# RWKV-7 chunk inverse: a direct product for the transposed matrix, half-width f16 copies into block-diagonal operands, and a new instruction order

## The chip, the cores and the metric

The kernel runs on one core of one Trainium2 chip (trn2). The metric is the device time of one execution in microseconds, as the median of several runs. The core has four engines that matter here. PE is the matrix engine, whose weight loads are listed apart as PEld. DVE is the vector engine, ACT the scalar engine and POOL the general engine. SP issues the transfers. Each engine runs its own instructions in a fixed order, and semaphores hold an instruction back until what it reads is there.

## What is computed

One layer of a streaming encoder: a projection feeds four HGRN2 heads and eight RWKV-7 heads, then come an output projection, cross attention over 256 memory rows, a SwiGLU block and the final norm. 1024 prompt tokens and 32 sample tokens go through it. The change touches the RWKV-7 recurrence alone:

```python
def rwkv7_mixer(p, shift0, s0, mu, w0, w_b, a0, a_b, g_b, k_k, k_a, r_k, gn_w, gn_b):
    ...
    a = jax.nn.sigmoid(a0 + ad @ a_b)
    kk = k * k_k
    k = k * (1.0 + (a - 1.0) * k_a)
    ...
    kk = kk / jnp.maximum(jnp.sqrt(jnp.sum(kk * kk, axis=-1, keepdims=True)), 1e-12)

    def step(S, xs_t):
        r_t, w_t, k_t, v_t, kk_t, a_t = xs_t
        sa = jnp.einsum('bhvk,bhk->bhv', S, -kk_t)
        S = (S * w_t[:, :, None, :] + sa[..., None] * (kk_t * a_t)[:, :, None, :]
             + v_t[..., None] * k_t[:, :, None, :])
        return S, jnp.einsum('bhvk,bhk->bhv', S, r_t)
```

The kernel computes it in chunks of 64 tokens. Inside a chunk the steps depend on each other through a strictly triangular 64x64 matrix A (token against token). The chunk needs the inverse of the identity minus A.

## The kernel before

The whole program is recorded as a graph (`Graph.record`) and laid out by a planner (`Graph.order`, `Graph.plan`) before it is emitted. So every instruction carries the line of the one emitting call, L384. The planner places instructions engine by engine. It uses estimated costs (`price`), a table of ranks, and perturbations of the ranks from the constants `START` and `NUDGE`. It packs buffers into regions of the on-chip memory: `f` and `mb` for most tiles, `r`, `rw` and `wr` for weights and rounded operands. These region names, and `bank` for the eight accumulator banks, are the names that a profile shows.

`mixers` runs `rwkv(0)`, two HGRN2 heads, `rwkv(2)` and two more HGRN2 heads. Beside them stand the projections that feed the second half, and later the key and value projections of the memory. The planner weaves these dense matmuls between the small ones, twelve at a time (`CUT = 4`, three matmuls each). `rwkv(j)` handles two pairs of heads (a pair fills the 128 partitions, 64 each) in five stages `s`. Four stages have 256 tokens, that is K = 8 chunks over the two pairs, and the last has 32 tokens and K = 2. That gives eight large stages and two small ones. One stage at a time may be in its first part (`AHEAD`, kind `rw`). A stage does the following.

- It forms the decayed operands. `ar[:, 0]` and `ar[:, 1]` hold the key direction and the receptance. `kbk[:, c, e]` holds, for head half e, the key direction times a, and the other slot holds k. The factor on k is formed by two tensor-scalar operations on POOL (`ka`, `oka`), followed by a multiply on POOL.
- Products of A: for each chunk and head half one f32 matmul, with 64 rows of weights, 128 columns of output and 128 moving columns (both parts of `ar` at once). It gives A, the k part of it, and the same for the receptance. DVE evacuates them through a mask in eight instructions of 256 columns into `am` and `aq`.
- `inverse(am, K)`: 16 small matmuls against the identity transpose A. DVE subtracts the result from the identity into the block-diagonal f32 tile `abd`, ACT copies that to f16 (`a16`), and POOL makes the first `xbd` from it. Then come five levels of doubling on f16 operands. In each, PE multiplies `a16` by y. DVE masks the result into p (`self.levs`, 512 columns) and again, twice as wide and with the zero halves, into the block-diagonal `pbd` (`place`, 1024 columns from the accumulator). PE multiplies `xbd` by p (the new y, copied by ACT) and `pbd` by x. DVE places that into `xbd`, again 1024 columns wide, and ACT copies it to x. At level 1 the product with x is made from both halves of `xbd` (`product_diag`, 16 matmuls in place of 8). A last f32 product corrects the result.
- The second part of the stage (kind `rc`) runs over its chunks one after another and ends with the group norm.

What the change touches: the constants at L38, `price` (L238 to L269), the masks in `constants`, the tile `diag` in `mixers`, the two `ka` instructions and the products of A in `rwkv`, and `inverse`.

Of the kernel before, what the change touches and what calls it, by code (L numbers as in the profile page):

```python
# [11 lines left out]
F32 = mybir.dt.float32  # L12
# [25 lines left out]
START, NUDGE = (3607, 1), ((80, 4396, 3), (130, 3947, 0.6), (150, 4396, 3), (265, 8110, 6), (275, 4333, 1.5), (340, 8895, 0.6), (380, 3280, 3), (405, 8085, 0.6), (410, 6339, 6), (420, 6614, 3), (430, 156, 0.2), (730, 4743, 12), (845, 2394, 1.5), (865, 156, 0.2), (870, 6104, 12), (875, 4027, 6), (895, 4109, 0.6), (900, 2031, 12), (905, 8539, 12), (930, 7618, 3), (950, 8689, 3), (965, 6104, 12), (975, 8050, 3), (985, 6104, 12), (1045, 8604, 12), (1060, 5136, 12), (1070, 4495, 1.5), (1255, 1, 0), (1295, 1462, 3), (1365, 8029, 1.5), (1430, 8194, 3), (1470, 9186, 0.2), (1530, 8029, 1.5), (1560, 8200, 1.5), (1630, 7663, 12), (1640, 7326, 3), (1700, 5100, 3), (1725, 629, 12), (1755, 5100, 3), (1760, 1728, 3), (1775, 4762, 6),)  # L38
# [188 lines left out]
def price(eng, method, args, kw):  # L227
# [39 lines left out]
    if method == "tensor_scalar":  # L267
        return 0.24 + n * (3.3e-3 if args[4] == ALU.max else 1.1e-3), 0.0
# [440 lines left out]
class Net:  # L709
# [5 lines left out]
    def constants(self):  # L715
# [33 lines left out]
        both = self.both = c.tile([128, 2, 64], F32, name="both")  # L749
        nc.vector.tensor_copy(both.rearrange("p h u -> p (h u)"), j64)  # L750

        def diagonal(m):

            d = c.tile([128, 2, 64], F32, name="levd")
            nc.vector.tensor_tensor(d, m.unsqueeze(1).to_broadcast([128, 2, 64]), both, ALU.mult)
            return d


        self.lev, self.levs = [], []
        for l in range(6):  # L760
# [10 lines left out]
            self.lev.append(diagonal(m) if l else m)  # L771
        self.lev0y = self.lev[0]
# [8 lines left out]
        self.lev0x = diagonal(m).rearrange("p h u -> p (h u)")  # L781
# [716 lines left out]
    def mixers(self):  # L1498
# [138 lines left out]
    def rwkv(self, j):  # L1637
# [8 lines left out]
        for s in range(5):  # L1646
# [72 lines left out]
            for a in range(2):  # L1719
                G.tensor_scalar(of(a_, a), of(a_, a), self.P("ka", j + a), self.P("oka", j + a), ALU.mult, ALU.add)  # L1720
# [13 lines left out]
            am, aq = ([self.w(t).rearrange("p (c u) -> p c u", c=8)[:, :K] for _ in half] for t in ("am", "aq"))  # L1734
# [26 lines left out]
            y1 = self.inverse(am, K)  # L1761
            akv = self.w("akv").rearrange("p (c u) -> p c u", c=8)[:, :K]
            ps = self.psm.tile([128, 8, 64], F32, tag="m", name="ps_ak")[:, :K]
            for c in range(K):
                PE.matmul(ps[0:64, c], lhsT=am[0][64:128, c], rhs=z[64:128, c, 0], start=True, stop=True)
                PE.matmul(ps[64:128, c], lhsT=am[1][0:64, c], rhs=z[0:64, c, 1], start=True, stop=True)
# [85 lines left out]
    def inverse(self, am, nc_):  # L1852
# [9 lines left out]
        abd = self.diag[self.diag_n % DIAG][:, :nc_]  # L1862
        self.diag_n += 1
        a16, xbd, pbd = (self.tmp([128, 8, 128], t, F16)[:, :nc_] for t in ("a16", "xbd", "pbd"))
# [14 lines left out]
        def product_diag(left, right):  # L1879

            ps = stacked()
            for c in range(nc_):
                PE.matmul(ps[:, c], lhsT=left[:, c], rhs=right[:, c, 0:64], start=True, stop=False)
                PE.matmul(ps[:, c], lhsT=left[:, c], rhs=right[:, c, 64:128], start=False, stop=True)
            nc.cut()
            return ps

        def halves_product(left, right):

            ps = stacked()  # L1890
            for c in range(nc_):
                for hf in half:
                    PE.matmul(ps[hf, c], lhsT=left[hf, c, hf], rhs=right[hf, c], start=True, stop=True)
# [209 lines left out]
```

## Time and profile before

| | |
|---|---|
| Three timed runs | 1793.56, 1795.97, 1800.94 us; median 1795.97 us |
| Span of the profiled execution, first to last instruction | 1792.9 us |
| Mean granted PE clock | 0.996 |
| Mixers (RWKV, HGRN2, projections, memory keys and values) | from about 95 to about 740 us of the span |
| Matmul records | 15639; f32 matmuls that are no transposes leave two records each |

The files give no time of the profiled execution other than its span, so sums are made against the 1792.9 us. The median of the runs is 3.1 us above that. A profile's group row reads: line, engine, operation, written tile and read tiles, shape, count, then the busy time in us and the mean of one in ns, then the idle time of the engine just before such instructions and who ended it. The mean length of a matmul is a latency, since matmuls overlap. What one costs is the busy time divided by the count.

### The profile page before, as it was taken

The page shows a single profiled execution, that of the slowest core. Times are in us where ns is not written, and L with a number is a line of the kernel's source. Part 1 is how long each engine was busy: PE and PEld are TensorE (multiplying, and loading weights), DVE is VectorE, ACT ScalarE, POOL GpSimd, SP SyncE. Part 2 cuts the span into 40 slices and gives each one's busy share as a digit, 9 for nine tenths or more (in the row PEclk, how much of TensorE's full clock was granted, in tenths as well). Part 3 has the DMA queues.
Part 4 walks back from the last instruction along what each step waited for, and adds up shares of the span by engine and source line. Part 5 has one row for each costly group of instructions (what it writes and reads, how often), then busy time and mean ns, then how long its engine had stood idle before and what let it go on. Part 6 is the DMA issues. An engine that isn't in the chain of part 4 may idle for free.

```text
span 1792.9 us, 39695 instructions
## 1 busy us (share of the span) xinstructions
PE 1753.3 (98%) x15639; PEld 1665.4 (93%) x15639; DVE 1289.6 (72%) x2538; ACT 854.3 (48%) x2025; POOL 575.1 (32%) x729
## 2 busy tenths in 40 slices
PE   7999999999999999999999999999999999999998
PEld 6998888898888888999999999999999999999997
DVE  6466668847768798424564557998777877979997
ACT  6745536656555677533333446333333333753432
POOL 5024325425524542153000037422322323233321
PEclk9999999999999999999999999999999999999999
DMA  5734323223412237743112233133222244645522
GB/s 186 226 110 113 108 63 97 79 85 97 120 56 68 60 92 246 240 138 105 48 49 70 90 115 96 57 123 114 90 98 98 95 141 152 184 142 158 185 84 98
DMA packets 212555, 205.06 MB, mean 114 GB/s; under 512 B 18808, under 2 KB 197616, under 8 KB 212368
## 3 DMA queue, kind: packets, MB, share of 16 engines
q1 hardware_dynamic: 212368, 202.52, 36.3%
q8 instruction: 123, 2.02, 0.5%
q14 instruction: 64, 0.52, 0.1%
HBM read 142.80 MB, written 59.67 MB: 113 GB/s over the span
## 4 chain that ended last, share of the span: by engine, by line
PE 79%; DVE 9%; ACT 3%; DMA 3%; POOL 3%; issue 3%; SPq 0%; DVEq 0%; ACTq 0%; POOLq 0%
PE bank L384 79%; DVE f L384 4%; DVE mb L384 2%; POOL f L384 1%; DVE rw L384 1%; DVE r L384 1%; ACT mb L384 1%; ACT f L384 1%; POOL mb L384 1%; DMA p_scratch<-mb 1%; DMA r<-h_scratch 1%; DMA mb<-in_x_prompt_dram 0%; ACT rw L384 0%; DMA f<-p_scratch 0%; DMA f<-out_dram 0%
## 5 line engine op out<-in xcount | busy, mean ns | idle before, releaser
L384 PE MATMUL bank<-r,rw 128*128 128x264 f32 (+1 forms) x5952 | 895.9, 305 | 1.5 <-DVE f L384 0.7
L384 PEld LDWEIGHTS bank<-r,rw 128*128 128x128 f32 x5952 | 840.3, 189 | 8.7 <-DVE rw L384 1.4
L384 PE MATMUL bank<-mb,rw 128*128 128x264 f32 (+3 forms) x3648 | 506.0, 293 | 2.7 <-ACT rw L384 0.9
L384 PEld LDWEIGHTS bank<-mb,rw 128*128 128x128 f32 x3648 | 481.2, 188 | 7.1 <-DVE rw L384 1.6
L384 DVE TENSOR_TENSOR f<-bank,f 128x264 f32<-128x264 f32 (+7 forms) x524 | 236.7, 466 | 161.1 <-PE bank L384 143.8
L384 ACT CAST rw<-wr 128x1024 fp32r<-128x1024 f32 (+3 forms) x168 | 119.7, 718 | 203.7 <-PE bank L384 176.8
L384 DVE TENSOR_TENSOR f<-f 128x264 f32<-128x264 f32 (+9 forms) x336 | 204.8, 628 | 13.4 <-ACT f L384 8.7
L384 POOL TENSOR_TENSOR f<-f 128x2 f32<-128x2 f32 (+8 forms) x201 | 112.6, 571 | 309.4 <-ACT f L384 260.6
L384 ACT ACTIVATE f<-f 128x256 f32<-128x256 f32 (+7 forms) x327 | 138.3, 445 | 119.8 <-DVE f L384 71.7
L384 PE MATMUL bank<-f 128*128 128x128 f32 (+13 forms) x1245 | 159.4, 275 | 4.6 <-DVE f L384 2.2
L384 DVE TENSOR_TENSOR mb<-bank,f 128x1024 f16<-128x1024 f32 (+5 forms) x191 | 135.3, 732 | 37.1 <-PE bank L384 32.2
L384 PEld LDWEIGHTS bank<-f 128*128 128x128 f32 (+5 forms) x1189 | 117.2, 159 | 24.0 <-DVE f L384 4.2
L384 DVE TENSOR_TENSOR rw<-wr,rw 128x512 fp32r<-128x512 f32 (+3 forms) x146 | 118.3, 816 | 28.1 <-ACT rw L384 24.3
L384 PE MATMUL bank<-f,mb 128*128 128x64 f16 (+5 forms) x2296 | 121.9, 218 | 15.8 <-DVE mb L384 14.2
L384 ACT CAST rw<-r 128x512 fp32r<-128x512 f32 (+2 forms) x111 | 63.2, 570 | 116.9 <-PE bank L384 90.6
L384 ACT COPY mb<-bank 128x512 f32<-128x512 f32 (+5 forms) x165 | 74.0, 462 | 70.2 <-PE bank L384 63.3
L384 ACT COPY f<-bank 128x264 f32<-128x264 f32 (+8 forms) x207 | 70.1, 356 | 53.5 <-PE bank L384 47.1
L384 DVE TENSOR_TENSOR rw<-r,rw 128x512 fp32r<-128x512 f32 (+2 forms) x111 | 77.7, 702 | 17.1 <-ACT rw L384 16.8
L384 PEld LDWEIGHTS bank<-f,mb 64*64 64x64 f32 (+4 forms) x1280 | 57.6, 140 | 30.5 <-DVE mb L384 16.2
L384 ACT CAST rw<-f 128x512 fp32r<-128x512 f32 (+3 forms) x71 | 45.9, 647 | 71.1 <-PE bank L384 64.6
L384 POOL TENSOR_TENSOR rw<-wr,rw 128x1024 fp32r<-128x1024 f32 x22 | 52.7, 2399 | 82.7 <-ACT rw L384 75.2
L384 PE MATMUL bank<-mb 64*64 64x64 f32 (+5 forms) x1516 | 73.4, 230 | 4.2 <-DVE mb L384 3.4
(121 smaller groups left out, 1818.8 us busy)
## 6 DMA issues: line engine op xcount, KB each, us to landing
wr<-in_w_in_dram SPq DMA_DIRECT2D x36, 512.0 KB
p_scratch<-mb SPq DMA_DIRECT2D x79, 176.0 KB
wr<-in_w_ff_dram SPq DMA_DIRECT2D x27, 512.0 KB
r<-in_w_ff_dram SPq DMA_DIRECT2D x25, 512.0 KB
f<-h_scratch SPq DMA_DIRECT2D x48, 264.0 KB
h_scratch<-f SPq DMA_DIRECT2D x16, 528.0 KB
f<-x_scratch SPq DMA_DIRECT2D x15, 528.0 KB
f<-p_scratch SPq DMA_DIRECT2D x60, 128.0 KB
```

Source lines behind the costliest of these rows:

```text
L384: getattr(eng, method)(*args, **kw)
```

## The change

Part by part:

- A is no longer made and then transposed. One set of 16 matmuls makes A transposed directly (`pst`, weights from `ar`, moving columns from `kbk`), and DVE copies it through a mask into `a32`, which starts as minus the identity (`copy_predicated`). A second set of 16 makes the k part (`psk`). A third, with 64 moving columns, makes the receptance part, first all chunks of one half, then all of the other (`pse`). Evacuations are 512 columns wide.
- `a32` is 64 columns wide per chunk. `xbd`, `pbd` and `abd` are three lasting f16 tiles, zeroed once. They are filled by two half-partition copies each: `a16` by ACT, `pbd` and `xbd` by DVE, from the f16 tiles p and x.
- `product_diag` is gone. x goes from the accumulator through ACT, and then by the two copies to `xbd`.
- The two `ka` instructions go to DVE.
- `price` gets entries for such copies and for POOL's tensor-scalar with two pointers. `START` and `NUDGE` get new numbers, so that the order of the whole program is another.

```diff
-START, NUDGE = (3607, 1), ((80, 4396, 3), (130, 3947, 0.6), (150, 4396, 3),
...
+START, NUDGE = (976, 1), ((20, 678, 0.6), (35, 5853, 0.6), (40, 8101, 3),
...
     if eng == "vector":
+        if method in ("tensor_copy", "tensor_scalar") and all(v.buf.space == "SB" for v in args[:2]):
+            return 0.135 + n * (0.26e-3 if out.dtype == args[1].dtype == F16 else 0.52e-3), 0.0
...
-        return 0.24 + n * (3.3e-3 if args[4] == ALU.max else 1.1e-3), 0.0
+        pointers = sum(isinstance(a, View) for a in args[2:])
+        return 0.24 + n * (3.3e-3 if args[4] == ALU.max else 4e-3 if pointers > 1 else 1.1e-3), 0.0
...
-            self.diag.append(self.sp.tile([128, 8, 128], F32, name="abd"))
-            nc.gpsimd.memset(self.diag[-1], 0.0)
+            self.diag.append(self.sp.tile([128, 8, 64], F32, name="a32"))
+            nc.vector.tensor_scalar(self.diag[-1], self.i64.unsqueeze(1).to_broadcast([128, 8, 64]), -1.0, None, ALU.mult)
+        self.bd = [self.sp.tile([128, 8, 128], F16, name=t) for t in ("xbd", "pbd", "abd")]
+        for t in self.bd:
+            nc.gpsimd.memset(t, 0.0)
...
             for a in range(2):
-                G.tensor_scalar(of(a_, a), of(a_, a), self.P("ka", j + a), self.P("oka", j + a), ALU.mult, ALU.add)
+                V.tensor_scalar(of(a_, a), of(a_, a), self.P("ka", j + a), self.P("oka", j + a), ALU.mult, ALU.add)
...
-            for a in range(2):
-                pse = [self.psm.tile([128, 4, 128], F32, tag="m", name="ps_a")[:, :m] for _ in half]
-                for c in range(m):
-                    for e, hf in enumerate(half):
-                        PE.matmul(pse[e][:, c], lhsT=kb[m * a + c][e], rhs=ar[hf, :, 64 * (m * a + c):64 * (m * a + c) + 64],
-                                  start=True, stop=True)
-                for e in range(2):
-                    for lst, o in ((am, 0), (aq, 64)):
-                        V.tensor_tensor(lst[e][:, m * a:m * a + m], pse[e][:, :, o:o + 64],
-                                        self.mask_a[:, o:o + 64].unsqueeze(1).to_broadcast([128, m, 64]), ALU.mult)
+            pst, psk, *pse = [self.psm.tile([128, 8, 64], F32, tag="m", name=t)[:, :K] for t in ("ps_at", "ps_am", "ps_aq", "ps_aq")]
+            a32 = self.diag[self.diag_n % DIAG][:, :K]
...
+                    PE.matmul(pst[hf, c], lhsT=ar[hf, 0, cc], rhs=kbk[hf, c, e], start=True, stop=True)
+            V.copy_predicated(a32, self.mask_t.unsqueeze(1).to_broadcast([128, K, 64]), pst)
...
+                    PE.matmul(psk[half[1 - e], c], lhsT=kbk[hf, c, 1 - e], rhs=ar[hf, 0, cc], start=True, stop=True)
+            V.tensor_tensor(am, psk, self.mask_a[:, 0:64].unsqueeze(1).to_broadcast([128, K, 64]), ALU.mult)
+            for e, hf in enumerate(half):
+                for c in range(K):
+                    PE.matmul(pse[e][:, c], lhsT=kb[c][e], rhs=ar[hf, 1, 64 * c:64 * c + 64], start=True, stop=True)
+                V.tensor_tensor(aq[e], pse[e], self.mask_a[:, 64:128].unsqueeze(1).to_broadcast([128, K, 64]), ALU.mult)
...
-        def place(dst, ps, mask):
-            V.tensor_tensor(dst.rearrange("p c (h u) -> p c h u", h=2),
-                            ps.unsqueeze(2).to_broadcast([128, nc_, 2, 64]),
-                            mask.unsqueeze(1).to_broadcast([128, nc_, 2, 64]), ALU.mult)
-
-        ps = stacked()
-        for c in range(nc_):
-            for e, hf in enumerate(half):
-                PE.matmul(ps[hf, c], lhsT=am[e][hf, c], rhs=self.ident[hf, hf], start=True, stop=True)
-        for hf in half:
-            V.tensor_tensor(abd[hf, :, hf], ps[hf], bc(self.i64[hf]), ALU.subtract)
+        def place(dst, src):
+            for hf in half:
+                V.tensor_copy(dst[hf, :, hf], src[hf])
+
...
-        S.copy(a16, abd)
-        G.tensor_tensor(xbd, abd, bc(self.lev0x), ALU.mult)
+        for hf in half:
+            S.copy(a16[hf, :, hf], a32[hf])
+        G.tensor_tensor(x, a32, bc(self.lev0x), ALU.mult)
+        place(xbd, x)
         V.tensor_tensor(y, product(a16, bc(self.i16)), bc(self.lev0y), ALU.mult)
         for l in range(1, 6):
             ps = product(a16, y)
             V.tensor_tensor(p, ps, bc(self.levs[l]), ALU.mult)
-            place(pbd, ps, self.lev[l])
+            place(pbd, p)
             S.copy(y32 if l == 5 else y, product(xbd, p))
-            ps = product(pbd, x) if l > 1 else product_diag(pbd, xbd)
-            place(xbd, ps, self.both)
-            if l < 5:
-                S.copy(x, ps)
+            S.copy(x, product(pbd, x))
+            place(xbd, x)
```

Three places in the order show it. The first is DVE in the first stage, from the halves of `kbk` (the 64x8x64 rows) to A. Before, eight masked evacuations (128x256) stand there, of which the last four are shown; the two rows in the last line build `abd` from the transposed A:

```order
L384 TENSOR_TENSOR mb_87<-bank_61,f_0_71 128x256
L384 TENSOR_TENSOR mb_87<-bank_58,f_0_71 128x256
L384 TENSOR_TENSOR mb_87<-bank_65,f_0_71 128x256
L384 TENSOR_TENSOR mb_87<-bank_63,f_0_71 128x256
L384 SCALAR_TENSOR_TENSOR mb_87<-bank_60,f_0_71,mb_87 128x319
L384 SCALAR_TENSOR_TENSOR mb_87<-bank_60,f_0_71,mb_87 128x31
L384 TENSOR_TENSOR rw_83<-wr_75,rw_83 128x1024
L384 TENSOR_TENSOR mb_87<-bank_64,f_0_71 64x8x64 x2
```

Now the same place on DVE: the `ka` pair (TENSOR_SCALAR), then A transposed straight into `a32` (COPY_PREDICATED), with the k part of `kbk` only behind it:

```order
L387 TENSOR_TENSOR mb_87<-mb_87 64x8x64 x2
L387 TENSOR_SCALAR mb_87<-mb_87,f_0_71 128x256 x2
L387 SCALAR_TENSOR_TENSOR mb_87<-bank_61,f_0_71,mb_87 128x31
L387 COPY_PREDICATED mb_87<-f_0_71,bank_63 128x512
L387 TENSOR_TENSOR mb_87<-mb_87 64x8x64
L387 TENSOR_TENSOR mb_87<-mb_87 128x512
L387 SCALAR_TENSOR_TENSOR mb_87<-bank_58,f_0_71,mb_87 128x351
L387 TENSOR_TENSOR mb_87<-bank_60,f_0_71 128x512
```

What moved: A no longer stands behind the k part and behind a transposing round through PE; one wide evacuation replaces ten narrower ones ahead of the inverse.

The second place is DVE inside the levels of the same inverse. Before, p (128x512) and the two places (128x1024) come from accumulator banks; the other rows are projections' evacuations and weight splits:

```order
L384 TENSOR_TENSOR f_0_71<-bank_62,f_0_71 128x512
L384 TENSOR_TENSOR mb_87<-bank_61,f_0_71 128x1024
L384 TENSOR_TENSOR f_0_71<-bank_61,f_0_71 128x512
L384 TENSOR_TENSOR mb_87<-bank_58,f_0_71 128x1024
L384 TENSOR_TENSOR rw_83<-wr_75,rw_83 128x1024
L384 TENSOR_TENSOR mb_87<-bank_63,f_0_71 128x1024
L384 TENSOR_TENSOR f_0_71<-bank_63,f_0_71 128x512
```

Now the copies (64x8x64, from region f to region mb, nothing from a bank) stand where the places stood:

```order
L387 COPY mb_87<-f_0_71 64x8x64 x2
L387 SCALAR_TENSOR_TENSOR mb_87<-bank_62,f_0_71,mb_87 128x351
L387 SCALAR_TENSOR_TENSOR mb_87<-bank_61,f_0_71,mb_87 128x351
L387 COPY mb_87<-f_0_71 64x8x64 x2
L387 TENSOR_TENSOR f_0_71<-bank_64,f_0_71 128x512
L387 COPY mb_87<-f_0_71 64x8x64 x2
L387 TENSOR_TENSOR rw_83<-wr_75,rw_83 128x1024
L387 COPY mb_87<-f_0_71 64x8x64 x2
L387 TENSOR_TENSOR f_0_71<-bank_62,f_0_71 128x512
```

What moved: each place became two copies between on-chip tiles, and the copies into `xbd` stand behind ACT's copy to x.

The third place is POOL in the first large stages. Before, two pairs of tensor-scalars, the second of them the `ka` pair, stand ahead of the multiply that makes k (128x512):

```order
L384 TENSOR_SCALAR mb_87<-mb_87,f_0_71 128x256 x2
L384 MEMSET mb_87 128x8
L384 TENSOR_SCALAR f_0_71<-f_0_71 128x256
L384 TENSOR_TENSOR f_0_71<-mb_87,f_0_71 128x128
L384 COPY f_0_71<-mb_87 128x8
L384 TENSOR_TENSOR f_0_71<-f_0_71 128x2x3
L384 TENSOR_SCALAR mb_87<-mb_87,f_0_71 128x256 x2
L384 TENSOR_TENSOR mb_87<-mb_87 128x512
```

Now only the first pair is left:

```order
L387 TENSOR_SCALAR mb_87<-mb_87,f_0_71 128x256 x2
L387 TENSOR_TENSOR f_0_71<-mb_87,f_0_71 128x128
L387 MEMSET mb_87 128x8
L387 TENSOR_TENSOR f_0_71<-mb_87,f_0_71 128x128
L387 COPY f_0_71<-f_0_71 128x8
L387 TENSOR_TENSOR f_0_71<-f_0_71 128x2x3
L387 TENSOR_TENSOR mb_87<-mb_87 128x512
```

What moved: POOL's multiply no longer has two tensor-scalars of its own in front of it.

More of the change, by code (lines that the diff above doesn't have):

```diff
@@ L747, in constants @@
             sel(m[hf, 64:128], [[1, 64]], 0, -1)
[L749 to L759, printed above, removed]
+        m = c.tile([128, 64], F32, tag="c1", name="mask_tf")
+        G.memset(m, 1.0)
+        for hf in half:
+            sel(m[hf], [[-1, 64]], -1, 1)
+        self.mask_t = c.tile([128, 64], mybir.dt.uint32, name="mask_t")
+        nc.vector.tensor_copy(self.mask_t, m)
+        self.levs = []
         for l in range(6):
@@ L770, in constants @@
             self.levs.append(m)
-            self.lev.append(diagonal(m) if l else m)
-        self.lev0y = self.lev[0]
+        self.lev0y = self.levs[0]
         m = c.tile([128, 64], F32, tag="lev0", name="lev")
@@ L780, in constants @@
         nc.vector.tensor_tensor(m, m, self.i64, ALU.subtract)
-        self.lev0x = diagonal(m).rearrange("p h u -> p (h u)")
+        self.lev0x = m
         mh = c.tile([128, 128], F32, tag="c1", name="mask_hf")
@@ L1760, in rwkv @@
             S.copy(z[0:64, :, 1], ps[0:64])
-            y1 = self.inverse(am, K)
+            y1 = self.inverse(a32, K)
             akv = self.w("akv").rearrange("p (c u) -> p c u", c=8)[:, :K]
@@ L1764, in rwkv @@
             for c in range(K):
-                PE.matmul(ps[0:64, c], lhsT=am[0][64:128, c], rhs=z[64:128, c, 0], start=True, stop=True)
-                PE.matmul(ps[64:128, c], lhsT=am[1][0:64, c], rhs=z[0:64, c, 1], start=True, stop=True)
+                PE.matmul(ps[0:64, c], lhsT=am[64:128, c], rhs=z[64:128, c, 0], start=True, stop=True)
+                PE.matmul(ps[64:128, c], lhsT=am[0:64, c], rhs=z[0:64, c, 1], start=True, stop=True)
             S.copy(akv, ps)
@@ L1850, in rwkv, with inverse @@
             nc.sync.dma_start(self.o_dram[:, 4 + j:6 + j, c0:c0 + n], y.rearrange("p (a n) -> p a n", a=2))
-    def inverse(self, am, nc_):
+    def inverse(self, a32, nc_):
         nc = self.nc
@@ L1861, in inverse @@
         half = (slice(0, 64), slice(64, 128))
-        abd = self.diag[self.diag_n % DIAG][:, :nc_]
-        self.diag_n += 1
-        a16, xbd, pbd = (self.tmp([128, 8, 128], t, F16)[:, :nc_] for t in ("a16", "xbd", "pbd"))
+        xbd, pbd, a16 = (t[:, :nc_] for t in self.bd)
         def bc(m):
@@ L1877, in product @@
             return ps
-        def product_diag(left, right):
-            ps = stacked()
-            for c in range(nc_):
[L1883 to L1886, printed above, removed]
         def halves_product(left, right):
```

19 lines of the change are left out of this document (13 added, 6 removed).

## The prediction, made before the changed kernel was run

> **What bounds the kernel now.** I read the page's busy line and its chain first, then the busy time by stretches of the span, then what the weight loads waited for.
>
> ```profile
> span 1792.9 us, 39695 instructions
> PE 1753.3 (98%) x15639; PEld 1665.4 (93%) x15639; DVE 1289.6 (72%) x2538; ACT 854.3 (48%) x2025; POOL 575.1 (32%) x729
> PE 79%; DVE 9%; ACT 3%; DMA 3%; POOL 3%; issue 3%; SPq 0%; DVEq 0%; ACTq 0%; POOLq 0%
> ```
>
> PE is busy for 98% of the span and carries 79% of the chain that ended last. So the time is PE's work plus the little that PE stands idle. DVE, with 9% of the chain, matters only where it holds PE up. The change lies in the mixers:
>
> ```profile
> 0.00:95.00 95.00, 79.06 (x496) 74.28 (x498) 54.59 (x107) 61.69 (x127) 34.56 (x86) 1.00 0.67 203
> 95.00:740.00 645.00, 633.54 (x7168) 565.16 (x7167) 469.49 (x996) 380.00 (x990) 244.16 (x391) 0.99 0.36 105
> 740.00:1540.00 800.00, 798.46 (x6054) 788.06 (x6053) 542.68 (x982) 300.84 (x650) 226.72 (x180) 1.00 0.31 101
> 1540.00:1793.00 253.00, 242.25 (x1928) 237.88 (x1926) 222.82 (x457) 111.74 (x258) 69.66 (x73) 0.99 0.47 147
> ```
>
> The columns are stretch, length, then busy us of PE, PEld, DVE, ACT and POOL. In the 645 us of the mixers PE is idle for only 645 - 633.5 = 11.5 us, but weight loads are absent for 80 us, because small matmuls come in bursts that wait for evacuations. Short waits hide under the tails of earlier matmuls, so the weight loads' own waits show them better. From 95 to 740 us they read:
>
> ```profile
> PEld bank L384 <- issue: 20.3, 76, 0.8
> PEld bank L384 <- DVE mb L384: 8.2, 12, 2.2
> PEld bank L384 <- DVE f L384: 6.1, 17, 1.2
> PEld bank L384 <- ACT mb L384: 3.5, 8, 1.1
> PEld bank L384 <- ACT f L384: 1.4, 6, 0.3
> ```
>
> Waits that DVE or ACT ended by a write into `mb` or `f`, where all tiles of the RWKV and HGRN2 parts lie, sum to 8.2 + 6.1 + 3.5 + 1.4 = 19.2 us. That is the most a shorter chain of small operations can give back in this stretch; the 20.3 us "issue" were ended by nothing that the change touches. The rest of the program, from 740 us on, keeps its instructions and only their order changes.
>
> **The change part by part: PE.** There are 8 stages with 16 small matmuls per product and 2 with 4, so 136 matmuls per kind. f32 ones leave two records each.
>
> ```profile
> L384 PE MATMUL bank<-f 64*128 64x128 f32 x128 | 9.1, 282 | 0.4 <-DVE f L384 0.4
> L384 PE MATMUL bank<-mb 64*128 64x128 f32 x112 | 8.6, 284 | 0.5 <-POOL mb L384 0.5
> L384 PE MATMUL bank<-f,mb 64*128 64x128 f32 x32 | 2.5, 282 | 0.0
> L384 PE MATMUL bank<-f,mb 64*64 64x64 f32 x976 | 38.2, 226 | 2.4 <-DVE mb L384 1.6 <-DVE f L384 0.7
> L384 PE MATMUL bank<-mb 64*64 64x64 f32 x728 | 28.6, 224 | 0.3 <-ACT mb L384 0.2
> L384 PE MATMUL bank<-f,mb 128*128 128x64 f16 x1016 | 51.6, 194 | 0.7 <-ACT mb L384 0.3
> L384 PE MATMUL bank<-mb 128*64 128x64 f32 x468 | 23.0, 231 | 3.4 <-DVE mb L384 3.4
> ```
>
> Removed: the products of A, three rows with 272 records, 9.1 + 8.6 + 2.5 = 20.2 us, or 149 ns a matmul. The transposing matmuls are 64x64: (38.2 + 28.6) / 1704 = 39 ns a record, 78 ns a matmul, 136 of them 10.6 us. `product_diag` loses 68 f16 matmuls at 51.6 / 1016 = 51 ns, 3.5 us. Together 34.3 us. Added: two sets of 136 matmuls of 64x64 at 78 ns, 21.2 us, and 136 for the receptance part, with 64 rows, 128 columns and 64 moving. The trace has no such f32 product. The bounds are 78 ns (the 64x64 ones) and 149 ns (the old products, with twice the columns); the 128*64 row gives 2 x 49 = 98 ns. The old products alternated between the two halves of the rows; the new ones run through one half at a time, so I go above 98 and take **120 ns**, 16.3 us. Added together 37.5 us. Net on PE **+3.2 us**; with the bounds -2.5 to +7.1.
>
> The row of the old products, 71 ns a record for 128 moving columns, is short beside 49 ns for the 64 of the 128*64 row. The Trainium skill (TensorEngine Tiling (Array Packing), Key Properties) says that different tiles of the array load and multiply in parallel. By it the new loop gives that parallelism up, and the product would stay at the old 149 ns and the sum at +7.1 us; no row here shows the same tile used in succession, so my 120 ns stands.
>
> **DVE, ACT and POOL.**
>
> ```profile
> L384 DVE TENSOR_TENSOR mb<-bank,f 128x1024 f16<-128x1024 f32 x75 | 91.3, 1220 | 26.0 <-PE bank L384 22.3 <-ACT mb L384 2.7 <-issue 0.6
> L384 DVE TENSOR_TENSOR f<-bank,f 128x512 f16<-128x512 f32 x56 | 38.2, 682 | 8.7 <-PE bank L384 8.6
> L384 DVE TENSOR_TENSOR mb<-bank,f 128x256 f32<-128x256 f32 x62 | 21.9, 410 | 2.6 <-PE bank L384 2.6
> L384 DVE TENSOR_TENSOR mb<-bank,f 64x512 f32<-64x512 f32 x16 | 11.0, 688 | 4.3 <-PE bank L384 4.1
> L384 DVE COPY mb<-bank 64x128 f32<-64x128 f32 x30 | 8.3, 277 | 15.4 <-PE bank L384 14.0 <-ACT mb L384 1.0
> L384 DVE TENSOR_SCALAR f<-f 128x256 f32<-128x256 f32 x32 | 11.1, 353 | 0.9
> L384 ACT CAST f<-bank 128x512 f16<-128x512 f32 x60 | 35.1, 585 | 48.9 <-PE bank L384 31.4 <-DVE mb L384 14.9 <-DVE f L384 2.1
> L384 POOL TENSOR_SCALAR mb<-mb,f 128x256 f32<-128x256 f32 x32 | 28.0, 882 | 16.8 <-DMA x_scratch<-mb 10.5 <-DVE mb L384 3.3 <-DMA mb<-p_scratch 2.5
> L384 POOL TENSOR_TENSOR mb<-mb 128x512 f32<-128x512 f32 x8 | 11.1, 1387 | 0.7
> ```
>
> A large stage loses ten places at 1220 ns (12.2 us), eight evacuations at 410 (3.3) and two subtractions at 688 (1.4). It gains four evacuations of 512 columns at 682 (2.7), 22 copies, and the two `ka` operations at 353 (0.7). The trace has no f16 copy between on-chip tiles. Its bounds are 277 ns (the 64x128 copy) and 688 (64x512 f32 from a bank). I take 353, the single-source operation that moves as many bytes per partition: 7.8 us. So DVE sheds 16.9 - 11.2 = 5.7 us a stage, 46 us in eight. Off the chain that is worth nothing, as PE covers it.
>
> The Trainium skill (VectorE: DVE Perf Modes, What auto-detection actually checks) puts a 16-bit copy from one on-chip tile to another in its fastest mode; for 512 columns its formula gives an estimate of about 0.29 us, which no run here shows yet.
>
> On the chain: ahead of the inverse, two `ka` operations (882 ns each) and the multiply (1387) on POOL no longer stand before A, nor does the round by the transposing matmuls with two subtractions, 2 x 0.88 + 1.39 + 2 x 0.69 = 4.5 us a stage. In a level, the path of x was p, place, product, place: 0.68 + 1.22 + 1.22 = 3.1 us outside PE. It becomes p, two copies, product, ACT's copy, two copies: 0.68 + 0.71 + 0.59 + 0.71 = 2.7 us, with one more hand-over between engines. Behind these copies DVE queues projections' evacuations, for which PE waits only when no bank is free. The path of y is as before. So a stage's first part gets 4.5 + 5 x 0.4 = 6.5 us shorter. PE fills most of that with dense matmuls, so it is worth only waits. DVE's share of a level falls from 3.1 to 0.68 + 4 x 0.353 = 2.1 us, by a third; I take a third off the 19.2 us of waits, **-6.4 us**. Bounds are -19.2 (all gone) and, since the new order may cover waits worse, +20 (twice today's).
>
> Costed at nothing: the extra ACT copy per stage, hidden because ACT is busy for 380 of 645 us, and worth 0.6 us a stage if it is not; two more memsets at the start, on a POOL that is busy for 35 of 95 us; the same transfers on SP's queue in another order.
>
> Sum: 1792.9 + 3.2 - 6.4 = 1789.7 us of span. The median of the runs is 3.1 us above this execution's span, so **1793 us**. My measure of no change is 0.5%, 9 us here, about what a measurement of this kernel can tell.
>
> **The rivals.** First, the two terms nearly cancel (the forecast). With PE between -2.5 and +7.1 and a fifth to a half of the waits gone (-4 to -10), the time lies between 1783.5 and 1799; it counts as no change down to 1787.
>
> Second, **the waits go nearly all**. If the 6.5 us per stage, 52 us over eight, let the new order keep dense work beside every hand-over, three quarters of 19.2 us vanish: 1796 + 3.2 - 14.4 = 1785 us. For it speaks that DVE is busy for 469 of 645 us; against it, that many of those waits belong to the HGRN2 heads and the serial second parts, which the change leaves alone.
>
> Third, **the copies queue behind POOL**, and PE waits longer than before. This is what such a collision looks like, POOL first, then DVE, then DVE's mean for that shape:
>
> ```profile
> 479.94 2.72 POOL L384 TENSOR_TENSOR rw<-wr,rw 128x1024 fp32r<-128x1024 f32 x1
> 480.49 2.80 DVE L384 TENSOR_TENSOR f<-f 128x256 f32<-128x256 f32 x2
> L384 DVE TENSOR_TENSOR f<-f 128x256 f32<-128x256 f32 x75 | 37.7, 509 | 4.8 <-ACT f L384 3.2 <-DMA f<-p_scratch 0.5 <-DMA out_dram<-f 0.4
> ```
>
> Two operations of 0.51 us took 2.80, until just after POOL ended. The old places, with one operand from a bank, average 1220 ns for 1024 columns and show no such stretch. If the copies do, the eleven pairs of a stage meet a busy POOL with a chance of 244 / 645 = 38%. A POOL instruction lasts 244 / 391 = 0.62 us on average, so 11 x 0.38 x 0.6 = 2.5 us a stage, 20 us in eight; half or all of it on PE gives 1796 + 3.2 + 10 = 1809 to 1819 us. It decides where a copy averages above some 0.5 us. The Trainium skill (SBUF — State Buffer, SBUF: two separate sides) says that a DVE operation in a two-port mode, or with two on-chip inputs, and a POOL operation exclude each other for a whole instruction. The two rows agree for two inputs; for copies no run shows it. Against it: POOL loses 16 tensor-scalars and half of each first `xbd`.
>
> That the change does not do what it says is no live case: the removed rows are gone from the order.
>
> **How the numbers follow.** Forecast 0.52, waits gone 0.29, copies behind POOL or worse cover 0.19. The likeliest is 1793. The range keeps the bounds of PE's term and reaches into both rivals: 1780 (1785 less the cheaper PE term, 5 us) to 1809. Faster by over 0.5% (under 1787) 0.31: the second rival with a little of the first. Slower by over 0.5% (above 1805) 0.18, the third almost whole. Within 0.5% 0.51.
>
> **What would show it.** PE's busy time in the mixers within a few us of 633.5; the new 64*128 64x64 product at 60 ns a record (39 to 75 are the bounds); f16 copies near 0.35 us, with a maximum under 0.7, or else the third rival; no 128x1024 f16 place; DVE some 46 us less busy; and the weight loads' waits on DVE and ACT at about 13 us where 19.2 were. Wrong if those waits fall under 6 us or pass 25, or if stretches after 740 us move by more than 5 us.

## The result, and the profile after

The changed kernel takes **1826.0 us** (median of 4 runs, 1825.4 to 1828.6) against 1796.1 us for the kernel before beside it. The ratio is 1.0166, 95% interval 1.0148 to 1.0183, so it is 30 us slower. The forecast of 1793 us was wrong, and so was its range, which ended at 1809.

The page of the changed kernel begins like this:

```profile
span 1826.9 us, 40186 instructions
PE 1780.2 (97%) x15843; PEld 1688.3 (92%) x15843; DVE 1256.8 (69%) x2613; ACT 857.3 (47%) x2045; POOL 547.8 (30%) x714
...
PE 36%; DVE 2%; issue 0%; ACT 0%; DMA 0%; DVEq 0%; POOL 0%; ACTq 0%
```

The chain that ended last could be followed through 38% of the span only, nearly all of it PE. DVE and POOL shed 33 and 27 us, as the change means them to. PE gained 27 us of busy time, and PE is what bounds the kernel. To see where, the span is cut where the first product of the output projection starts, at 737 us before and at 764 us after. First the busy times by stretch of the kernel before, then of the changed one (stretch, length, then PE, PEld, DVE, ACT, POOL):

```profile
95.00:737.00 642.00, 630.54 (x7150) 562.42 (x7149) 466.93 (x993) 378.28 (x988) 244.16 (x391) 0.99 0.35 105
737.00:1792.90 1055.90, 1043.71 (x7997) 1028.67 (x7995) 768.06 (x1440) 414.30 (x911) 296.38 (x253) 1.00 0.35 112
```

```profile
95.00:764.00 669.00, 654.77 (x7316) 584.97 (x7312) 434.42 (x1068) 383.39 (x1012) 221.11 (x373) 0.99 0.36 108
764.00:1826.90 1062.90, 1046.31 (x7995) 1028.87 (x7993) 767.25 (x1441) 414.15 (x912) 291.87 (x253) 1.00 0.35 111
```

The mixers grew by 27 us, of which 24.2 us are PE's busy time and 2.8 us are idle. The rest, with the same instructions in another order, grew by 7 us. What the weight loads waited for between 95 and 767 us:

```profile
PEld bank L387 <- issue: 17.9, 68, 0.8
PEld bank L387 <- DVE mb L387: 6.6, 13, 1.1
PEld L387 <- DVE mb L387: 5.7, 8, 2.1
PEld bank L387 <- DVE f L387: 5.3, 14, 0.8
PEld bank L387 <- ACT f L387: 3.9, 9, 1.3
PEld bank L387 <- ACT mb L387: 2.4, 7, 0.8
PEld L387 <- ACT mb L387: 1.1, 4, 0.5
```

The waits that DVE or ACT ended by a write into `mb` or `f` sum to 25.0 us. Before, from 95 to 740 us, there were these three beside the 19.2 us of the prediction's four rows:

```profile
PEld L384 <- DVE mb L384: 1.0, 4, 0.3
PEld L384 <- DVE f L384: 0.7, 2, 0.4
...
PEld L384 <- ACT mb L384: 0.3, 1, 0.3
```

That makes 21.2 us. They grew by 4 us, where the forecast took 6.4 us off them. By the four rows with `bank` that the prediction summed, they went from 19.2 to 18.2 us. The rise lies in the rows without `bank`, from 2.0 to 6.8 us; these are the f16 weight loads, which read `xbd`, `pbd` and `abd`.

Next the groups that the prediction asked for: the receptance products and the f16 copies of the changed kernel, each with count, busy us and mean ns, and the view of the tile `mb` with minimum, median and maximum of the copies' ns.

```profile
L387 PE MATMUL bank<-f 64*128 64x64 f32 x257 | 24.7, 259 | 0.8 <-DVE f L387 0.4 <-ACT mb L387 0.3
L387 PE MATMUL bank<-mb 64*128 64x64 f32 x80 | 9.7, 283 | 0.5 <-POOL mb L387 0.5
L387 PE MATMUL bank<-mb,f 64*128 64x64 f32 x32 | 4.0, 275 | 0.0
L387 PE MATMUL bank<-f,mb 64*128 64x64 f32 x40 | 2.5, 236 | 0.0
```

```profile
L387 DVE COPY mb<-f 64x512 f16<-64x512 f16 x166 | 64.2, 394 | 25.4 <-ACT f L387 22.8 <-PE bank L387 0.2
L387 DVE COPY mb<-mb 64x512 f16<-64x512 f16 x10 | 4.9, 486 | 0.2
```

```profile
L387 DVE COPY mb<-f x200: 176/286/2508, 97.2 to 695.5; 64x512 f16<-64x512 f16 x83, 64x128 f16<-64x128 f16 x17
```

The four PE rows hold 409 records and 40.9 us. 137 of the records are transposes of the same shape, which the kernel before has in two rows:

```profile
L384 PE MATMUL bank<-f,mb 64*128 64x64 f32 x72 | 3.5, 231 | 0.0
L384 PE MATMUL bank<-f 64*128 64x64 f32 x65 | 3.3, 228 | 0.0
```

That leaves 40.9 - 6.8 = 34.1 us for 272 records, **125 ns a record** where 60 was forecast and 75 was the upper bound. The view's median of 286 ns is over 200 copies of both widths, but the 154 copies of 64x512 that last under 350 ns have the same median. The other 22 last up to 2.5 us: 64.2 + 4.9 - 176 x 0.286 = 18.8 us of DVE's time is beyond the median.

Two stretches of the timelines show both (start, length, engine, what, count). First eight receptance products of the changed kernel (16 records), all on one half. Then sixteen of them (32 records) with alternating halves, from the run e3_alternate below. Then sixteen products of A of the kernel before, with 128 moving columns and alternating halves:

```profile
170.46 2.00 PE L387 MATMUL bank<-f 64*128 64x64 f32 x16
```

```profile
174.91 2.00 PE L387 MATMUL bank<-f 64*128 64x64 f32 x32
```

```profile
226.37 2.05 PE L384 MATMUL bank<-f 64*128 64x128 f32 x32
```

Eight on one half take as long as sixteen that alternate. In the traces the products on one half start 223 ns apart. Those that alternate start in pairs, 6 or 7 ns apart, and the pairs follow each other after the same 223 ns, so that a product takes 112 ns on average. 64 moving columns cost as much as 128.

And a blocked pair of copies in the changed kernel:

```profile
183.23 0.58 DVE L387 COPY mb<-f 64x512 f16<-64x512 f16 x2
...
185.30 2.37 POOL L387 TENSOR_TENSOR rw<-wr,rw 128x1024 fp32r<-128x1024 f32 x1 [10.15 <-ACT rw L387]
185.30 2.81 DVE L387 COPY mb<-f 64x512 f16<-64x512 f16 x2
...
188.17 0.41 PE L387 MATMUL bank<-f,mb 128*128 128x64 f16 x8 [1.38 <-DVE mb L387]
```

Two copies take 0.58 us in one place and 2.81 in the other, where they start together with a POOL operation of 2.37 us. PE then stands idle for 1.38 us, until they are done.

### The profile page after: what moved, and what is told of

Same layout as the page of the kernel before. It is cut to its first block, busy times and chain, and to the rows that moved or that the text cites. A ratio compares the mean times of both kernels' runs of the same rounds, so it can differ in the third digit from the quotient of the medians.

```text
span 1826.9 us, 40186 instructions
## 1 busy us (share of the span) xinstructions
PE 1780.2 (97%) x15843; PEld 1688.3 (92%) x15843; DVE 1256.8 (69%) x2613; ACT 857.3 (47%) x2045; POOL 547.8 (30%) x714
## 5 line engine op out<-in xcount | busy, mean ns | idle before, releaser
L387 DVE TENSOR_TENSOR f<-bank,f 128x264 f32<-128x264 f32 (+5 forms) x508 | 226.8, 460 | 177.9 <-PE bank L387 154.4
L387 POOL TENSOR_TENSOR f<-f 128x64 f32<-128x64 f32 (+8 forms) x214 | 125.2, 598 | 330.3 <-ACT f L387 260.6
L387 DVE TENSOR_TENSOR f<-f 128x264 f32<-128x264 f32 (+8 forms) x325 | 195.6, 624 | 21.8 <-ACT f L387 14.8
L387 PE MATMUL bank<-f 128*128 128x128 f32 (+10 forms) x1613 | 178.9, 264 | 6.0 <-DVE f L387 2.4
L387 PEld LDWEIGHTS bank<-f 128*128 128x128 f32 (+6 forms) x1613 | 139.9, 153 | 30.8 <-issue 8.5
L387 PE MATMUL bank<-f,mb 128*128 128x64 f16 (+6 forms) x2113 | 115.2, 216 | 19.5 <-DVE mb L387 17.9
L387 ACT COPY mb<-bank 128x352 f32<-128x352 f32 (+6 forms) x154 | 69.3, 462 | 88.3 <-PE bank L387 76.2
L387 DVE TENSOR_TENSOR rw<-r,rw 128x512 fp32r<-128x512 f32 (+2 forms) x118 | 87.3, 743 | 32.5 <-ACT rw L387 32.0
L387 ACT COPY f<-bank 128x264 f32<-128x264 f32 (+7 forms) x220 | 76.0, 363 | 65.2 <-PE bank L387 55.2
L387 DVE COPY mb<-f 64x512 f16<-64x512 f16 (+1 forms) x200 | 70.9, 360 | 30.9 <-ACT f L387 27.1
L387 PE MATMUL bank<-mb,f 64*64 64x64 f32 (+7 forms) x610 | 80.3, 306 | 1.0 <-ACT mb L387 1.0
```

The lines of the kernel that those rows point to most:

```text
L387: getattr(eng, method)(*args, **kw)
```

## The experiments

Theory 1: the receptance products run on one half of the array at a time and so cost twice. Theory L: the copies stand behind POOL. The rival to both: the new order as such. "Order kept" means that the edit is made where the instructions are emitted, after the planner. Each run's distance is that of its median from the kernel before beside it; the changed kernel's own is 29.9 us. The intervals reach 2 to 6 us to either side, so smaller differences between two runs are not told apart.

| run | median us | before beside it | ratio, 95% interval | distance us |
|---|---|---|---|---|
| e1_quarters | 1815.6 | 1794.9 | 1.0129, 1.0109 to 1.0148 | 20.8 |
| e2_before_halves | 1793.0 | 1794.9 | 0.9993, 0.9977 to 1.0010 | -1.8 |
| e3_alternate | 1873.0 | 1794.9 | 1.0442, 1.0420 to 1.0465 | 78.1 |
| e4_merged | 1854.7 | 1794.9 | 1.0346, 1.0319 to 1.0372 | 59.8 |
| e5_before_halves | 1797.2 | 1794.3 | 1.0018, 1.0007 to 1.0029 | 2.9 |
| e6_no_copies | 1816.0 | 1794.3 | 1.0122, 1.0107 to 1.0137 | 21.7 |
| n_after | 1852.7 | 1794.3 | 1.0329, 1.0313 to 1.0346 | 58.4 |
| n_before | 1824.5 | 1794.3 | 1.0166, 1.0151 to 1.0182 | 30.2 |
| e7_late_on_act | 1817.9 | 1794.3 | 1.0135, 1.0113 to 1.0157 | 23.6 |
| e9_others_on_act | 1828.4 | 1794.3 | 1.0183, 1.0150 to 1.0216 | 34.1 |
| e8_quarters_no_copies | 1799.9 | 1794.3 | 1.0032, 1.0019 to 1.0045 | 5.6 |
| e10_merged_priced | 1813.8 | 1793.8 | 1.0109, 1.0090 to 1.0128 | 20.0 |
| e11_alternate_priced | 1812.3 | 1793.8 | 1.0109, 1.0089 to 1.0129 | 18.6 |
| e12_quarters_late_on_act | 1812.9 | 1796.5 | 1.0086, 1.0071 to 1.0101 | 16.3 |
| e13_alternate_late_on_act | 1812.0 | 1796.5 | 1.0089, 1.0072 to 1.0106 | 15.4 |
| e14_after_no_pool1024 | 1818.4 | 1794.3 | 1.0142, 1.0120 to 1.0165 | 24.1 |
| e15_before_no_pool1024 | 1797.4 | 1794.3 | 1.0022, 1.0007 to 1.0038 | 3.1 |

**The receptance products.** e1_quarters, at the emitting call:

```diff
+if method == "matmul" and lhsT is f32 64x128 and rhs is 64x64:
+    for m in (slice(0, 64), slice(64, 128)):
+        eng.matmul(args[0][m], **{**kw, "lhsT": kw["lhsT"][:, m]})
+    continue
```

> The changed kernel with each receptance product (64 rows, 128 columns, 64 moving, f32) issued as two products of 64x64 at the very same place; the order of everything on every engine is the changed kernel's. Theory 1 (the same half of the array used in succession): in the changed kernel these 136 products start 223 ns apart, 33 us in all, against the 120 ns of the prediction; 64x64 products on alternating tiles start 59 ns apart, so 272 of them take 16 us and the time falls by 15 to 18 us, to 1808 to 1811. Theory 2 (the order and the waits on DVE and ACT made the loss; the products' length is hidden): within 4 us of 1826.

The distance fell from 29.9 to 20.8 us with every instruction else in its place. That lies between the ranges of the two theories: 9 us, where theory 1 asked for 15 to 18 and theory 2 for 4 at most. The quarters do start 58 ns apart on average in the trace, 117 ns a product. But the shorter products cover less of what PE waits for. Busy times by stretch:

```profile
95.00:753.00 658.00, 638.11 (x7552) 568.84 (x7552) 434.15 (x1068) 382.40 (x1010) 217.66 (x372) 0.99 0.36 109
```

PE's busy time in the mixers fell by 16.7 us (654.8 to 638.1), the stretch by 11. PE's idle time rose from 14.2 to 19.9 us, and the weight loads' waits of the kind summed above from 25.0 to 31.7.

The same loop shape put into the kernel before. e2_before_halves and e5_before_halves, order kept:

```diff
+if all matmuls of a node are the 64x128 products of A:
+    calls = sorted(calls, key=lambda c: c[2]["lhsT"].region()[0])
```

> The kernel before with its products of A (64 rows, 128 columns, 128 moving) run, inside each group of eight, first all on one half of the rows and then all on the other; nothing else differs. Theory 1: 136 products go from 112 ns (149 ns with the change-over) to 223 ns or more each, the time rises by 10 to 16 us, to 1806 to 1812. Theory 2: no change, within 4 us of 1796.

> The kernel before with its products of A (64 rows, 128 columns, 128 moving) run, inside each group of eight, first the four on one half of the rows and then the four on the other; nothing else differs. Theory 1 (a product on the same half as the one ahead starts 223 ns after it, whatever the moving columns): three of four products go from 112 to 223 ns or more, 102 x 0.11 = 11 us, so 1805 to 1809. Theory 2 (the length of these products is hidden): within 4 us of 1796.

In the first of the two the condition looked for operands of 64x128 where they are 64x2x64, so nothing was sorted. Its program is that of the kernel before, and it only shows how well a repeat agrees. In the second the products did run in fours:

```profile
L387 PE MATMUL bank<-f 64*128 64x128 f32 x128 | 12.1, 285 | 0.0
L387 PE MATMUL bank<-mb 64*128 64x128 f32 x112 | 10.7, 287 | 0.0
L387 PE MATMUL bank<-f,mb 64*128 64x128 f32 x32 | 2.8, 285 | 0.0
```

They cost 25.6 us instead of 20.2, and the time rose by 2.9 us: a third or less of the 9 to 13 us that theory 1 expected, and inside the range of the rival. The trace has two streams of records, each with 111 or 112 ns between them, so a half still takes 223 ns for a product and 0.89 us for four. But each run of four starts 554 ns after the run ahead of it on the other half, and so runs beside its end: 139 ns a product, not 223. The changed kernel's runs of eight stand apart, with nothing of the other half near, in seven of the eight large stages. So this run bears out the price of a half, but its total can't tell the two theories apart.

e3_alternate and e4_merged change the program, so the planner lays a new order:

```diff
-for e, hf in enumerate(half):
-    for c in range(K):
+for c in range(K):
+    for e, hf in enumerate(half):
         PE.matmul(pse[e][:, c], lhsT=kb[c][e], rhs=ar[hf, 1, ...])
```

```diff
-psk and pse[e]: products of 64 moving columns
+PE.matmul(pse[e][:, c], lhsT=kb[m * a + c][e], rhs=ar[hf, :, ...])   # 128 moving, halves alternate
```

> The changed kernel with the receptance loop going through both heads of a chunk before the next chunk, so that the halves alternate; the planner lays a new order. Theory 1: the products start 112 ns apart, 16 us in all, and the time is 1826 - 16 = 1810, with up to 10 us either way from the new order. Theory 2: 1816 to 1836, the order alone deciding.

> The changed kernel's inverse and its own transposed product, but the key part and the receptance part of A again from one product of 128 moving columns with alternating halves, as before. Theory 1: the 33 us of the receptance products and some 9 us of the key products give way to 20 us, so 22 us less: 1804, with up to 10 us either way from the new order. Theory 2: above 1815.

Theory 1 missed both by 40 us and more. e4 lies in the range of theory 2, which was open above 1815, and e3 37 us beyond it. The receptance products of e3_alternate do fall from 33.0 to 16.6 us by their starts in the trace. But the shifts in `NUDGE` go by the numbers of the nodes; in another program they hit other nodes, and the order got worse by more than the gain: the changed kernel without any shift, n_after below, stands at 58.4 us, and these two at 78.1 and 59.8. They tell nothing of the total.

**The order.** n_after and n_before have `START, NUDGE = (0, 0), ()`.

> The changed kernel with an empty NUDGE and START (0, 0), so with the planner's order as it comes without any of the 41 shifts. Theory O (the loss of 30 us lies in the particular order): it stands less than 15 us from the kernel before with the same empty table. Theory P (the loss lies in the changed parts): 25 to 40 us above that kernel. Both expect it above 1826, by 10 to 50 us.

> The kernel before with the same empty table, for comparison with n_after. Both theories expect it above 1796, by 10 to 50 us; what counts is the distance between the two: under 15 us for theory O, 25 to 40 for theory P.

Without the shifts the two kernels stand 28.2 us apart, with them 29.9. That is what theory P expected, that the loss lies in the changed parts. It is one pair of orders, and not a clean one: the granted clock was 0.983 to 0.987 in n_after's runs and 0.991 to 0.993 in n_before's. If all of PE's 1793 us stretched with the clock, that 0.7% would make some 12 of the 28 us (an estimate from these figures). What carries the argument is the runs at a kept order. The shifts are worth 30.2 us to the kernel before and 58.4 - 29.9 = 28.5 to the changed one.

**The copies.** e6_no_copies leaves out `tensor_copy` into `xbd` and `pbd`. e7_late_on_act and e9_others_on_act make 23 of them `real.scalar.copy`. Order kept in all three.

> The changed kernel without the 220 narrow copies into the two block-diagonal operands, which keep their zeros; order as in the changed kernel. Theory A (the copies, 22 of which end just behind a POOL operation, hold PE up): 15 to 25 us less, 1801 to 1811. Theory B (the dense work covers the copies, the loss is the receptance products and the rest of the order): at most 6 us less, 1820 to 1826.

> The changed kernel with 23 of the 220 narrow copies, those that last over 0.35 us in its trace (22 of them end some 0.15 us behind a POOL operation), made by ACT instead of DVE; the order is kept. Theory L (the copies cost time because DVE stands still behind a POOL operation, 20 us of DVE's time in all): 6 to 12 us less, 1814 to 1820. Theory C (each copy costs by standing in the chain, blocked or not): within 3 us of 1826.

> The control of the run before: 23 other copies, none of which waits for POOL in the changed kernel's trace, made by ACT. Theory L: no gain, 1823 to 1832. Theory C, or a DVE that is merely too full: the same as with the 23 blocked ones.

All copies together are worth 8 us (29.9 to 21.7), less than theory A asked for and more than theory B. The 23 long ones, moved away, gave 6 us. 23 others, moved likewise, gave nothing (34.1 against 29.9 us, within the intervals). Between the two, run side by side, lie 10 us, and every run with the long ones moved (1817.4 to 1822.4 us) was faster than every run with the others moved (1822.5 to 1832.2). So it is the blocked copies. e7 took only a part of the blocking away: in its trace 12 other copies of 64x512 last over 350 ns, and the time beyond 286 ns a copy fell from 19.9 us (by the single copies) to 13.8; in e9 it stayed at 20.0.

e14_after_no_pool1024 and its control take the blocking operations away instead, order kept:

```diff
+if node.eng == "gpsimd" and method == "tensor_tensor" and out is fp32r with 1024 columns:
+    real.scalar.copy(args[0].real(), args[1].real())
+    continue
```

> The changed kernel with POOL's 22 subtractions of 1024 columns (2.4 us each, weight rounding in the mixers) replaced by copies on ACT, so that the subtraction's low part is wrong and POOL is idle in those places; the order is kept. Theory L (the copies blocked behind POOL cost time): the longest copies go, their excess falls from 20 us to under 8, and the kernel gains 5 to 10 us more than the kernel before does by the same edit. Otherwise both move alike, within 3 us of each other.

> The control: the kernel before with the same edit. It has no f16 copies for POOL to block, only operations with two on-chip operands. Theory L: 0 to 4 us less than 1796. Otherwise the same as in the changed kernel.

The copies of e14_after_no_pool1024, by groups and by the view of the tile:

```profile
L390 DVE COPY mb<-f 64x512 f16<-64x512 f16 x166 | 48.0, 296 | 31.9 <-ACT f L390 25.5 <-PE bank L390 4.0
```

```profile
L390 DVE COPY mb<-f x200: 175/286/1179, 96.0 to 684.7; 64x512 f16<-64x512 f16 x83, 64x128 f16<-64x128 f16 x17
```

The first row's mean fell from 394 to 296 ns, and all 176 copies of 64x512 together spend 1.8 us beyond 286 ns each. The changed kernel gained 5.8 us, the kernel before lost 3.1. Theory L expected 5 to 10 us between them; it is 8.9, close to the 8.2 us of all copies, and each of the two figures is uncertain by some 5 us. Within that, blocking makes up about all of what the copies cost.

**Both at once.**

> Both at once: the receptance products as 64x64 quarters, and without the 220 narrow copies. If the two costs are separate, their gains add: 1826 - 10.4 - 10.0 = 1805.6, so 1802 to 1809, the first out_proj product stands where it stood before (737 us, within 4), and what is left of the loss lies behind it. If one covers the other, 1810 to 1816.

```profile
95.00:738.00 643.00, 633.21 (x7582) 565.99 (x7577) 360.17 (x848) 381.99 (x1011) 219.79 (x373) 1.00 0.37 112
738.00:1798.60 1060.60, 1045.54 (x7994) 1028.53 (x7992) 768.55 (x1441) 413.85 (x912) 296.30 (x253) 1.00 0.34 112
```

1799.9 us, 2 us below the range that was set: the gains are 9.1 and 8.2 us alone and 24.3 together, so each cost had in part covered the other. The first out_proj product stands at 738 us, as before. In these mixers PE is busy for 2.7 us longer than in the kernel before, about the +3.2 of the forecast, and idle for 1.7 us less. The 5 us that are left lie behind it, where the order alone differs.

**Versions with all work kept.** The planner of e10 and e11 is told of the blocking, and each got shifts of its own:

```diff
 def shares_port(eng, method, args):
+    if eng == "vector" and method in ("tensor_copy", "tensor_scalar") and all(v.buf.space == "SB" for v in args[:2]):
+        return True
```

> The changed kernel's inverse with its copies; the key part and the receptance part again from one product with alternating halves (as in e4_merged); the planner told that DVE's on-chip copies and tensor-scalars exclude POOL's two-input operations; and its order shifted by a table of its own, as both kernels have one. Theory 1 (the loss is the one-half loop and the copies blocked behind POOL, both unknown to the planner): with both gone the mixers end at about 737 us as before, the f16 copies average under 0.31 us, and the time is 1788 to 1804. Theory P' (the new chain with its copies is dearer in itself): 1810 or more.

> The same with the changed kernel's three sets of products, the receptance loop alternating between the heads, and a table of its own. Theory 1: receptance products 112 ns apart, copies under 0.31 us on average, and some 6 us of PE work more than in e10_merged_priced: 1794 to 1812. Theory P': 1815 or more.

> e1_quarters with the 22 copies that last over 0.35 us in its own trace made by ACT; no work is left out and the order is the changed kernel's. Theory L with theory 1: the gains of e1_quarters (10) and e7_late_on_act (8) add: 1826 - 18 = 1808, within 4. If the quarters leave the blocked copies covered: 1813 to 1817, as e1_quarters.

> e11_alternate_priced with the 27 copies that last over 0.35 us in its own trace made by ACT: the blocked copies tested in another order. Theory L: 4 to 9 us less than 1812, so 1803 to 1808. Otherwise within 3 us of 1812.

All four are faster than the changed kernel by 10 to 15 us, and none beats the kernel before. The 64x512 copies of e10 and of e11:

```profile
L389 DVE COPY mb<-f 64x512 f16<-64x512 f16 x176 | 61.6, 353 | 25.4 <-ACT f L389 21.4 <-POOL f L389 1.0
```

```profile
L389 DVE COPY mb<-f 64x512 f16<-64x512 f16 x176 | 66.2, 378 | 19.1 <-ACT f L389 16.2
```

By their times e10 speaks for the dearer chain and e11 lies on the edge. The first out_proj product stands at 748 and 752 us, not at 737. But their copies average 353 and 378 ns, not under 310: copies met POOL operations all the same, though the planner was told (20 of e10's 23 and 24 of e11's 25 that last over 350 ns end some 0.15 us behind one). So they do not test the chain with free copies. e12 and e13 missed. Moving the blocked copies to ACT gave 4 and 3 us by the distances where 8 and 4 to 9 were expected, and only 2.7 and 0.4 us by the medians; e13's 1812.0 us is what its "otherwise" expected. In both traces other copies are blocked in their place: 12 and 11 on DVE last over 350 ns, 12 and 10 of them ending just behind a POOL operation, and the time beyond 286 ns a copy is 15.7 us in e12 (20.4 in e1) and 8.3 in e13 (16.2 in e11). And on ACT such a copy lasts twice as long, as e7 shows:

```profile
L390 ACT COPY mb<-f 64x512 f16<-64x512 f16 x20 | 12.3, 616 | 3.2 <-DVE f L394 2.1 <-POOL f L394 0.8
```

Whether the new inverse could beat the old one with copies that POOL cannot block stays open.

## Why the prediction was wrong

- **PE's work, +3.2 us: this step failed.** It failed at "The old products alternated between the two halves; the new ones run through one half at a time, so I go above 98 and take 120 ns". 136 products were to cost 16.3 us and cost 34.1. The upper bound of 149 ns, "with twice the columns", was none: it took the moving columns for what a product costs, while 64 and 128 of them cost the same, and the half that a product occupies for 223 ns sets the price. The old row was cheap because two halves worked at once. The Trainium skill (TensorEngine Tiling (Array Packing), Key Properties) says just that, that different tiles load and multiply in parallel. The prediction weighed it, drew 149 from it and kept 120; the runs agree with the rule, and the price is 251 ns by busy time.
- **PE's other terms** were sized about right: the removed products are 20.2 us by their rows, the rows of 64x64 products in the mixers grew by 8.8 us (80.2 to 89.0) where 21.2 - 10.6 = 10.6 were forecast, and those of f16 products shrank by 3.7 (61.3 to 57.6) where 3.5 were. So of the 24.2 us that PE's busy time grew by in the mixers, 34.1 - 16.3 = 17.8 us are this one mis-sized term, and 3.2 were forecast.
- **The waits, -6.4 us**, rose by 4 (21.2 to 25.0): this second term failed too, in its sign. The rise goes with the blocked copies. With the blocking nearly gone they are 19.4 us (e14), against 23.9 in the kernel before with the same edit (e15); with copies and one-half loop gone they are 19.4 (e8), against 21.2. So the shorter chain was worth 2 to 4 us of the 6.4. In e8 it shows as 1.7 us less idle time of PE, and the 2.7 us of added work use that up.
- **The third rival came true beside the first error.** It was priced at 20 us of DVE's time, and 18.8 were measured. That match is luck in part: the price has 88 pairs of copies that meet POOL with a chance of 38%, so 33 meetings of 0.6 us, and the trace has 22 long copies at 0.9 us beyond the median each, nearly all of it in 12 of them, behind POOL operations of 1.5 to 2.6 us. It set two tests that disagree. "Where a copy averages above some 0.5 us" was not met; the mean was 394 ns, but a mean hides 22 copies among 176. "A maximum under 0.7, or else the third rival" pointed the right way: the longest took 2.5 us. Some 8 to 10 us of it reached the end (e7 against e9, and e14 against e15). The Trainium skill (SBUF — State Buffer, SBUF: two separate sides) has a DVE copy in a two-port mode and a POOL operation exclude each other for a whole instruction; the timeline at 185.30 us and e14 agree, with 2.81 us for two copies of 0.29. The median of 286 ns also meets the estimate of 0.29 us worked out from the Trainium skill (VectorE: DVE Perf Modes, The TRN2 errata); the prediction's 353 was too long for a free copy.
- **DVE, 46 us less busy:** 32.5 in the mixers (466.9 to 434.4). The blocked copies took 18.8 us, and the free ones, at 286 ns where 353 was taken, gave back 11.8; that leaves some 6 us that no run here accounts for.
- **Behind 740 us** "under 5 us" was forecast. It moved by 7, and by 5 in e8, with the same instructions. That leaves the order; which of its pieces was not tried.

## What to carry to other kernels

Before splitting a small product, look at which part of the array each piece uses and in what sequence: a loop over one half, here with half the moving columns, can cost more than the product that it replaces (34.1 us against 20.2), and the busy time per record of an alternating loop is no bound for it. Judge copies between on-chip tiles by their longest, not their mean, wherever POOL works beside DVE. An order tuned for one program is worth some 30 us here and was lost with each edit that changed the program (e3, e4), so compare edits at a kept order, or both kernels without the tuning.

## What was not expected of the hardware

- An f32 product of 64 rows and 128 columns keeps its half of the rows for 223 ns, with 64 as with 128 moving columns. Products on the two halves run side by side, two in the same 223 ns. As two products of 64x64 on the two column halves it takes 117 ns, without any alternation of the rows (e1).
- In runs of four per half (e5), a run starts 554 ns after the run ahead of it on the other half, while that run lasts 0.89 us. PE works ahead into the other half when its products stand close enough.
- A free f16 copy of 64x512 takes 286 ns on DVE and 616 ns on ACT. Of the 22 in the changed kernel that last over 350 ns, 20 end 141 to 150 ns behind the POOL operation that they meet.
